# A Strassen-like trunk kernel on one core: one raw tile more, one low less, and more sums done by accumulating transfers

## The chip, the core and the metric

The kernel runs on one core of a Trainium2 chip. The core has five engines with an instruction stream each: TensorE (PE, with its weight loads shown apart as PEld), VectorE (DVE), ScalarE (ACT), GpSimd (POOL) and SyncE (SP). They work from on-chip memory of 128 partitions; sixteen DMA engines move data between it and HBM, and also from one place of it to another. Transfers are issued on queues of SyncE, ScalarE and GpSimd; only those of GpSimd are used here with an add at the destination. The metric is the device time of one launch in microseconds, lower is better.

## The reference

Only layer 0 runs (`DEPTH = 1`): an RMS norm, a stick-breaking attention branch, the residual add, and the final norm. All in float32, with 256 rows, width 4096 and 32 heads of 128.

```python
xn = rms_norm(x, norm_attn)
q, k, v, g = split(xn @ w_in_attn, 4)        # (256, 4096) @ (4096, 16384)
z = q @ k.T / sqrt(128)                      # per head, strictly causal
a = exp(log_sigmoid(z) + suffix sums of log_sigmoid(-z))
h = x + ((a @ v) * silu(g)) @ w_out_attn     # (256, 4096) @ (4096, 4096)
out = rms_norm(h, final_norm)
```

Nearly all arithmetic is in the two products with the weights. The weights are 256 MB for the first product and 64 MB for the second.

## The kernel before

**Products in three passes.** Float32 numbers are split into a high part in the fast format float32r (`wh`, `sh`, `oh`) and a low part that is the rest (`wl`, `sl`, `ol`). One product (`mm3`, line 909) is three matmuls of 512 columns: high x high, low weight x high, high weight x low. For each weight tile ScalarE casts the high part (`cast`, line 556; in the profile `wh<-raw`) and VectorE subtracts it from the raw tile (`low`, line 571; `wl<-raw,wh`).

**Units, steps and parts.** The output columns are cut into 16 input units of 1024 columns (256 each of q, k, v and gate, so two heads) and 4 output units of 1024. A unit goes over the 4096 inner rows in 8 steps. The first unit of each product is plain; the others treat the four 256-column blocks and the two halves of rows as 2 x 2 block products. A seven-product step (`SEVEN_PARTS`, line 97; steps 1, 3, 4, 6 of an input unit, 1, 3, 6 of an output unit) needs seven products for each of its two pairs of inner rows instead of eight, but some of its weight tiles are sums of raw tiles. A mixed step (0, 2, 5) does that for half of its rows, and the remaining steps are ordinary (`EIGHT_PARTS`). A step of seven parts has 14 products, a mixed one 15, an ordinary one 16. A part is the use of one low tile: two products in a seven-product step, four in an ordinary one. Each unit collects its results in seven PSUM banks; at its end VectorE and ScalarE combine the banks (`combine`, line 805; `qk_sb`, `gv_sb`), and the banks are needed again by the next unit.

**Raw tiles and sums.** `load` (line 427) brings in the four quarter tiles of each step on SyncE's queue, two DMAs of 256 KB per tile, into a ring `raw` of `RAW_BUFS` places. In a seven-product step, `add_block` (line 467) adds a second block onto the tile (1, 0) by an accumulating transfer from HBM on GpSimd's queue; it is called T3. That tile is loaded `EARLY` = 2.5 tiles ahead of its turn. `sums` (line 496) then makes further weights in place on VectorE: `near - far`, the second sum and the third sum (`raw<-raw,raw` in the profile). For steps listed in `FOURTH_IN` and `FOURTH_OUT` the third sum is instead an accumulating transfer from on-chip memory to on-chip memory on GpSimd's queue (`raw<-raw`, T4):

```python
fourth = not mixed and parts[a]["s"] in (FOURTH_IN if parts[a]["u"] < OUT0 else FOURTH_OUT)
...
def moved_third():
    yield nc.until(("lows", b))
    x, y = raw[(q, 0, 1)], raw[(q, *near)]
    yield moved("gpsimd", lambda: nc.gpsimd.dma_start(x, y, accum_op=ALU.add), ...)
    yield nc.until(("T4", q), lead=T3_LEAD)
    nc.tell(("sums", g[0]))
    tile_done(q, 0, 1)
    tile_done(q, *near)
```

A raw tile's place comes free when its last cast, low and sum are done. The sixth and seventh part of a seven-product step (`LATE_FROM`, `LATE_BEHIND`) run behind the second part of the step that follows.

**Rings.** Besides `raw` there are `PAIRS` = 6 places for cast tiles and `LOWS` = 6 for lows; a place is given back when TensorE has finished the part. A raw tile and a low both take 4 KB of each partition. `KEPT` (lines 48, 352 to 358): the last parts of the kernel keep their tiles, and their products are ordered by bank, first banks 4 and 5, then 2, then 3, so that row block 1 is complete before row block 0 and its norm and output can begin (`last_h`, line 1208; `finish`, line 1291). `KEPT` must not exceed the number of lows.

**A written order.** The class `Plan` (line 139) plays the kernel through at build time with a cost for each operation and transfer, and writes down the instructions of each engine in the order in which the played engines take them, by a key (how urgent a piece is) among those that are ready. On the chip each engine executes its list strictly in order, waiting on semaphores. So the constants touched by the change act in two ways: some set how many places or transfers there are, and others (`T3_LEAD`, `TEN_WAIT`, `QK_LEAD`, `SPREAD`) only shift the order of the lists. `T3_LEAD` is the time after an accumulating transfer's landing before what needs it may be listed. `TEN_WAIT` (line 399) is the time between an attention matmul's being ready and its being listed on TensorE; `QK_LEAD` (line 1037) the same for a unit's first attention step. A transfer with an add is booked with 1.78 us per 256 KB, a plain one with 0.83 (line 265).

**Attention.** The two heads of a unit are worked out during the next unit: five groups of small matmuls per head on TensorE (`tr`, `z`, the suffix sums into `z`, the gate's transpose, `o`), with ScalarE and VectorE between them. The result goes to HBM (`spill`), and `blocks_of_heads` (line 1064) fetches it back (`p<-spill`, GpSimd's queue) and splits it into the stationary forms `oh` and `ol` of the second product. `SPREAD` says from which half-step on: form `s` is not begun before half-step `int(SPREAD[0] + SPREAD[1] * s)`, counted from the start of the last input unit, of 16 half-steps in a unit.

Of the kernel before, what the change touches and what calls it, by code (L numbers as in the profile page):

```python
# [42 lines left out]

SEVEN_IN, MIX_IN = (1, 3, 4, 6), (0, 2, 5)
SEVEN_AFTER, MIX_AFTER = (1, 3, 6), (0, 2, 5)
RAW_BUFS = 8
PAIRS, LOWS = 6, 6
KEPT = 6
LAST_STEPS = (2, 6, 5, 1, 0, 3, 7, 4)
LATE_FROM, LATE_BEHIND = 4, 1  # L50

SPREAD = (8, 1.1)
HEADS_AHEAD = 3
HEADS_LATER = 12
AHEAD, SUMS_AHEAD = 1.0, 3.0
PIPE = 1
T3_LEAD = 1500
FOURTH_IN, FOURTH_OUT = (1, 3), ()
FOURTH_AHEAD = 6.0
RAW_LEAD = 0  # L60
EARLY = 2.5
TEN_WAIT = 1200
QK_LEAD = 2000
CAST_AHEAD = 3.0
BLOCKS_LATER = 2
OUT_ACT = (1, 4, 7)
# [68 lines left out]
def tensor_ns(n):  # L135
    return 0.4167 * n + 13.4 if n > 128 else 109.0
# [137 lines left out]
def kernel(  # L274
# [76 lines left out]
    n_parts = len(parts)  # L351
    kept = range(n_parts - KEPT, n_parts)
    begun = len(PLAIN_PARTS) * NS
    order = [(n, k) for n in range(begun) for k in range(len(parts[n]["prods"]))]
    order.sort(key=lambda e: (parts[e[0]]["s"], parts[e[0]]["prods"][e[1]][2]))
    order += [(n, k) for n in range(begun, n_parts - KEPT) for k in range(len(parts[n]["prods"]))]
    for banks in ((4, 5), (2,), (3,)):
# [41 lines left out]
    def ten(emit, *n):  # L399
        return nc.work("tensor", 90 + sum(tensor_ns(m) for m in n), emit, nc.here - 1e4, wait=TEN_WAIT)  # L400

# [10 lines left out]
    for name, places in (  # L412
        ("raw", RAW_BUFS), ("w", PAIRS), ("low", LOWS), ("gh", 3), ("one", 1), ("two", 1),
        ("qkh", 1), ("qkl", 1), ("f", 1), ("att", 1), ("heads", 1),
# [12 lines left out]
    def load():  # L427
# [8 lines left out]
        for _, q, t, k in sorted(tiles):  # L436
            if 1 < q < NS:
                yield nc.until(("used", 0, max(HALF * q - LOAD_AHEAD, 0)))
            yield nc.take("raw")
            raw[q, t, k] = wp.tile([P, HG, HALF, CW], F32, tag="raw", name=f"raw{q}_{t}{k}", bufs=RAW_BUFS)  # L440
            if seven[q] and (t, k) == (1, 0):
# [54 lines left out]
    def sums(q):  # L496
# [16 lines left out]

        yield nc.until(("T3", q), lead=T3_LEAD)
        yield nc.until(("lows", a))
# [9 lines left out]
        def moved_third():  # L525
# [5 lines left out]
            )  # L531
            yield nc.until(("T4", q), lead=T3_LEAD)
            nc.tell(("sums", g[0]))
# [358 lines left out]
    def gate(u):  # L892
        yield nc.until(("gv", u))
        g = st["gv", u][:, :, CW:W]
        n = NT * CW
        yield nc.take("qkl")
        l = ap.tile([P, NT, CW], F32, tag="qkl", name=f"gl{u}")
        yield act(lambda: nc.scalar.activation(l, g, AF.Abs), n)
        yield act(lambda: nc.scalar.activation(l, l, AF.Exp, scale=-1.0), n)
        yield act(lambda: nc.scalar.activation(l, l, AF.Ln, bias=1.0), n)  # L900
        yield dve(
            lambda: nc.vector.scalar_tensor_tensor(out=l, in0=g, scalar=0.0, in1=l, op0=ALU.min, op1=ALU.subtract), n
        )
        yield act(lambda: nc.scalar.activation(l, l, AF.Exp), n)
        yield dve(lambda: nc.vector.tensor_tensor(out=g, in0=g, in1=l, op=ALU.mult), n)
        nc.give("qkl")
        nc.tell(("gate", u))
# [127 lines left out]
    def heads(u):  # L1035
        nc.start(gate(u))
        yield nc.until(("qk", u), lead=QK_LEAD)
        for i in range(HG):
# [21 lines left out]
    def later_than(u, s):  # L1060
        s = int(SPREAD[0] + SPREAD[1] * s)
        return "used", u + s // FINE, s % FINE
# [56 lines left out]
    def fetch():  # L1119

        yield nc.until("loaded", ("h", NJ - 3, 1))
        for c in AWAY:
            yield nc.take("raw")
            both = wp.tile([P, HG, HALF, CW], F32, tag="raw", name=f"back{c}", bufs=RAW_BUFS)
            for t in range(NT):
# [318 lines left out]
```

## Time and profile before

| | us |
|---|---|
| three timed runs | 1742.09, 1746.84, 1747.45 |
| their median | 1746.84 |
| the profiled execution | 1742.72 |
| its span, first to last instruction | 1741.0 |

The profile shows one execution. It gives, for each engine, busy time and instructions; for windows of time, each engine's busy time with the number of instructions, then the granted TensorE clock as a share of full speed, the share of the sixteen DMA engines' time that was busy (it can come out a little over 1), and the rate in GB/s; for each group of instructions, which engine waited for what (in all, how often, longest); for DMA issues, their size and the median time from issue to landing; and the chain of work that ended last. Matmuls are pipelined, so one that lasts 0.39 us can be followed by the next after less. A wait in square brackets behind a timeline row is the idle time of that engine before the instruction, with what ended it. Since nearly every instruction is issued through one helper, all have line 158; rows are told apart by their tiles, written as out<-in.

### The profile page before, as it was taken

How to read it: one execution, taken by the hardware profiler on the slowest of the kernel's cores; microseconds unless marked ns; L12 is line 12 of the kernel's file. 1: busy time of each engine (PE TensorE's matmuls, PEld its weight loads, DVE VectorE, ACT ScalarE, POOL GpSimd, SP SyncE). 2: the span in 40 equal slices, each digit the busy share in tenths (PEclk: the TensorE clock that was granted, in tenths of full speed). 3: DMA queues.
4: the chain of work that ended last, by engine and by line, in shares of the span. 5: the costliest groups of instructions: out<-in, count | busy, mean ns of one | idle time of the engine just before them, and what ended most of it. 6: DMA issues, size and time to landing. Idle time of an engine off the chain costs nothing.

```text
span 1741.0 us, 23954 instructions
## 1 busy us (share of the span) xinstructions
PE 1713.9 (98%) x7690; PEld 1407.4 (81%) x7690; DVE 1630.2 (94%) x1872; ACT 1227.0 (70%) x1599; POOL 209.1 (12%) x224
## 2 busy tenths in 40 slices
PE   9999999999999999999999999999999999999997
PEld 6888888888888888888787878787888778888885
DVE  7889999999999999999999999999999987899997
ACT  7876777676777676767686767676767665666664
POOL 0010111011101011111111111111111022011100
PEclk9999999999999999999999999999999999999998
DMA  9998989888989898988888988889898778798886
GB/s 302 316 251 242 254 243 241 239 252 254 243 253 248 249 239 254 238 252 236 250 242 246 237 250 232 247 235 260 232 258 236 254 251 241 232 290 243 261 255 230
DMA packets 240543, 434.84 MB, mean 250 GB/s; under 512 B 25472, under 2 KB 45440, under 8 KB 240416
## 3 DMA queue, kind: packets, MB, share of 16 engines
q1 hardware_dynamic: 197616, 354.24, 62.0%
q0 software_dynamic: 41504, 77.22, 24.4%
q10 hardware_dynamic: 1296, 1.85, 0.3%
q8 instruction: 60, 0.98, 0.2%
q14 instruction: 67, 0.55, 0.1%
HBM read 407.52 MB, written 9.96 MB: 240 GB/s over the span
## 4 chain that ended last, share of the span: by engine, by line
PE 65%; DVE 13%; DMA 11%; issue 5%; ACT 4%; SPq 1%; POOL 0%; ACTq 0%; DVEq 0%; POOLq 0%
PE acc L158 62%; DMA raw<-in_w_in_dram 8%; DVE wl L158 8%; ACT wh L158 3%; DVE raw L158 3%; PE z L158 2%; DMA xres<-in_x_dram 1%; PE o L158 1%; SPq L158 1%; DMA p<-spill 1%; PE tr L158 1%; DMA raw<-in_w_out_dram 1%; ACT f L158 0%; DVE qk_sb L158 0%; DVE h L158 0%
## 5 line engine op out<-in xcount | busy, mean ns | idle before, releaser
L158 ACT CAST wh<-raw 128x1024 fp32r<-128x1024 f32 (+1 forms) x959 | 941.9, 1021 | 393.1 <-DMA raw<-in_w_in_dram 201.2
L158 DVE TENSOR_TENSOR wl<-raw,wh 128x1024 fp32r<-128x1024 f32 (+1 forms) x959 | 1100.8, 1184 | 60.3 <-ACT wh L158 57.0
L158 PE MATMUL acc<-wh,sh 128*128 128x512 f32 x1883 | 751.6, 399 | 4.3 <-DVE qk_sb L158 2.5
L158 PE MATMUL acc<-wl,sh 128*128 128x512 f32 x1883 | 735.9, 391 | 6.7 <-DVE wl L158 6.0
L158 PE MATMUL acc<-wh,sl 128*128 128x512 f32 x1883 | 735.6, 391 | 0.0
L158 PEld LDWEIGHTS acc<-wl,sh 128*128 128x128 f32 x1883 | 354.5, 188 | 85.2 <-DVE wl L158 15.7
L158 PEld LDWEIGHTS acc<-wh,sh 128*128 128x128 f32 x1883 | 354.2, 188 | 77.0 <-DVE qk_sb L158 5.8
L158 PEld LDWEIGHTS acc<-wh,sl 128*128 128x128 f32 x1883 | 353.8, 188 | 75.5 <-DVE sl L158 0.2
L158 DVE TENSOR_TENSOR raw<-raw,raw 128x1024 f32<-128x1024 f32 (+1 forms) x339 | 326.2, 964 | 2.0
L158 POOL DMA_DIRECT2D raw<-in_w_in_dram x105 | 127.9, 1218 | 931.6 <-DMA raw<-in_w_in_dram 522.9
L158 PE MATMUL acc<-wl,oh 128*128 128x512 f32 x485 | 189.5, 391 | 2.2 <-DVE wl L158 2.1
L158 PE MATMUL acc<-wh,oh 128*128 128x512 f32 x485 | 189.9, 391 | 0.0
L158 PE MATMUL acc<-wh,ol 128*128 128x512 f32 x485 | 188.8, 389 | 0.0
L158 PEld LDWEIGHTS acc<-wl,oh 128*128 128x128 f32 x485 | 91.1, 188 | 23.2 <-DVE wl L158 4.8
L158 PEld LDWEIGHTS acc<-wh,ol 128*128 128x128 f32 x485 | 91.1, 188 | 18.8
L158 PEld LDWEIGHTS acc<-wh,oh 128*128 128x128 f32 x485 | 91.1, 188 | 18.7
L158 ACT ACTIVATE f<-f 128x384 f32<-128x384 f32 x96 | 50.5, 526 | 3.0
L158 POOL DMA_DIRECT2D raw<-raw x30 | 26.5, 882 | 208.9 <-ACT f L158 86.7
L158 ACT CAST oh<-p 128x512 fp32r<-128x512 f32 (+3 forms) x41 | 19.3, 488 | 32.5 <-DVE p L158 16.6
L158 POOL DMA_DIRECT2D raw<-in_w_out_dram x18 | 21.5, 1192 | 136.2 <-DMA raw<-in_w_out_dram 105.4
L158 DVE SCALAR_TENSOR_TENSOR gv_sb<-acc,rin_v,gv_sb 128x512 f32<-128x512 f32 x45 | 33.5, 745 | 0.7
L158 POOL DMA_DIRECT2D p<-spill x41 | 22.9, 567 | 90.4 <-DVE ol L158 84.7
(88 smaller groups left out, 749.3 us busy)
## 6 DMA issues: line engine op xcount, KB each, us to landing
raw<-in_w_in_dram SPq DMA_DIRECT2D x1016, 256.0 KB, 5.0
raw<-in_w_out_dram SPq DMA_DIRECT2D x256, 256.0 KB, 5.1
raw<-in_w_in_dram POOLq DMA_DIRECT2D x60, 512.0 KB, 8.7
raw<-raw POOLq DMA_DIRECT2D x30, 512.0 KB, 6.8
raw<-in_w_in_dram POOLq DMA_DIRECT2D x45, 256.0 KB, 6.3
p<-spill POOLq DMA_DIRECT2D x41, 128.0 KB, 4.7
raw<-in_w_out_dram POOLq DMA_DIRECT2D x9, 512.0 KB, 8.8
xr<-in_x_dram SPq DMA_DIRECT2D x16, 256.0 KB, 5.5
```

What stands on the lines that cost most here:

```text
L158: return self.tc.keep_in_program_order(getattr(self.engine, name)(*args, **kw))
```

## The change

Only constants differ. There is one more raw tile and one low less; the last five parts are reordered instead of six; the third sum of step 4 of the 15 input units that have seven-product steps, and of step 1 of the three such output units, becomes an accumulating transfer; and four constants of the planner are shifted: forms of heads begin two half-steps later, what follows an accumulating transfer is listed 0.5 us later, attention matmuls are listed 0.2 us earlier after being ready, and a unit's first attention step 0.5 us earlier. The change was described with the words "weights of the first product loaded first" as well; the difference between the two files has no line for it.

```diff
-RAW_BUFS = 8
-PAIRS, LOWS = 6, 6
-KEPT = 6
+RAW_BUFS = 9
+PAIRS, LOWS = 6, 5
+KEPT = 5
...
-SPREAD = (8, 1.1)
+SPREAD = (10, 1.1)
...
-T3_LEAD = 1500
-FOURTH_IN, FOURTH_OUT = (1, 3), ()
+T3_LEAD = 2000
+FOURTH_IN, FOURTH_OUT = (1, 3, 4), (1,)
...
-TEN_WAIT = 1200
-QK_LEAD = 2000
+TEN_WAIT = 1000
+QK_LEAD = 1500
```

## The prediction

> **What bounds the kernel now.** I read the busy shares first, then the windows of 100 us, then the waits of the weight loads, the chain, and the timeline where the chain leaves TensorE.
>
> ```profile
> span 1741.0 us, 23954 instructions
> ...
> PE 1713.9 (98%) x7690; PEld 1407.4 (81%) x7690; DVE 1630.2 (94%) x1872; ACT 1227.0 (70%) x1599; POOL 209.1 (12%) x224
> ```
> ```profile
> 0.00:100.00 100.00, 96.05 (x405) 76.35 (x406) 80.04 (x148) 82.66 (x155) 4.83 (x11) 0.98 0.92 304
> 500.00:600.00 100.00, 100.00 (x455) 82.84 (x454) 97.17 (x102) 73.38 (x91) 11.85 (x11) 1.00 0.88 246
> 1100.00:1200.00 100.00, 98.84 (x444) 80.49 (x443) 94.53 (x101) 72.42 (x90) 11.85 (x11) 1.00 0.86 242
> 1300.00:1400.00 100.00, 98.10 (x446) 80.37 (x444) 95.79 (x115) 73.96 (x98) 13.59 (x19) 1.00 0.83 243
> ```
>
> Three resources are nearly full at once: TensorE at 98 to 100 in 100 us, VectorE at 95 to 97, the DMA engines at 0.83 to 0.92 (second last column). From 500 to 600 us TensorE has no hole and VectorE is at its fullest. Where TensorE has holes, VectorE is a little emptier: it is late there because it was held up before. So TensorE sets the end, and what can be won is its holes.
>
> How much is that? A hole shows best in the weight load that ends it (waits of the whole run; then of the window from 97 to 1300 us; then the timeline at one hole):
>
> ```profile
> PEld acc L158 <- DVE wl L158: 20.5, 30, 1.1
> PEld acc L158 <- DVE qk_sb L158: 5.8, 9, 1.1
> ```
> ```profile
> PEld acc L158 <- DVE wl L158: 10.5, 17, 1.1
> ```
> ```profile
> 1111.14 0.39 PE L158 MATMUL acc<-wh,sh 128*128 128x512 f32 x1
> 1111.66 1.22 DVE L158 TENSOR_TENSOR raw<-raw,raw 128x1024 f32<-128x1024 f32 x1
> 1111.80 0.19 PEld L158 LDWEIGHTS acc<-wl,sh 128*128 128x128 f32 x1 [0.69 <-DVE wl L158]
> ```
> ```profile
> 1095.21 5.31 DMA raw<-in_w_in_dram
> ...
> 1115.85 15.82 PE acc L158 x68
> ...
> 1443.06 51.72 PE acc L158 x228
> ```
>
> The last chain line gives the undisturbed pace: 51.72/228 = 0.227 us for a 512-column matmul. At 1111 us the next matmul starts 0.66 us after the one before, so 0.43 us is lost where the weight load waited 0.69: a wait costs 0.26 less than it reads. That makes 20.5 - 30 x 0.26 = 12.7 us behind lows (`wl`), of them 10.5 - 17 x 0.26 = 6.1 in the input units up to 1300 us, and 5.8 - 9 x 0.26 = 3.5 us behind evictions (`qk_sb`): **16.2 us** or 0.9% in all. No change of order can win more.
>
> Where are they? The loss at 1111 us lies in step 6 (a seven-product step) of an input unit. The chain has just come out of a DMA load at 1095; the timeline shows how:
>
> ```profile
> 1099.93 5.37 ACT L158 CAST wh<-raw 128x1024 fp32r<-128x1024 f32 x6 [3.96 <-DMA raw<-in_w_in_dram]
> ...
> 1101.96 5.24 DVE L158 TENSOR_TENSOR wl<-raw,wh 128x1024 fp32r<-128x1024 f32 x5 [1.26 <-ACT wh L158]
> ```
>
> ```profile
> L158 ACT CAST wh<-raw 128x1024 fp32r<-128x1024 f32 (+1 forms) x959 | 941.9, 1021 | 393.1 <-DMA raw<-in_w_in_dram 201.2
> ```
>
> That is no single case: loads hold the casts up for 201 us of the run. ScalarE stands 3.96 us for a raw tile, VectorE then 1.26 us for the cast, and ten microseconds later TensorE has its hole. VectorE cannot make good what it lost, because a seven-product step asks too much of it:
>
> ```profile
> 1339.98 4.63 DVE L158 TENSOR_TENSOR wl<-raw,wh 128x1024 fp32r<-128x1024 f32 x4
> ```
>
> Four in 4.63 us with the last taking 1.22 is one per 1.14 us. A step with four sums on VectorE needs 7 lows and 4 sums, 11 x 1.14 = 12.5 us, against 14 products x 3 x 0.227 = 9.5 us on TensorE. Steps 3, 4 and 6 run it down; steps 7, 0 and 2 refill it.
>
> **The change part by part.**
>
> *Third sums by transfer* (step 4 of 15 input units, step 1 of 3 output units). Removed: 18 VectorE sums of 1.14 us, 20.5 us of VectorE, of which 1.14 per input unit falls just ahead of the losing step 6. The same sum in steps 1 and 3 already goes that way, 30 times. Added are 18 GpSimd issues and their transfers:
>
> ```profile
> raw<-raw POOLq DMA_DIRECT2D x30, 512.0 KB, 6.8
> ```
> ```profile
> q0 software_dynamic: 41504, 77.22, 24.4%
> ```
> ```profile
> 1073.50:1081.60 8.10, 8.10 (x39) 6.75 (x38) 6.67 (x8) 5.02 (x8) 1.19 (x1) 1.00 1.06 269
> 1081.60:1092.10 10.50, 10.50 (x50) 8.69 (x49) 10.21 (x11) 8.74 (x12) 1.21 (x2) 1.00 0.73 207
> 1092.10:1104.30 12.20, 12.20 (x55) 10.13 (x54) 10.72 (x12) 7.81 (x10) 0.59 (x1) 1.00 0.91 266
> 1104.30:1117.00 12.70, 11.68 (x49) 8.72 (x49) 12.15 (x13) 8.61 (x11) 1.16 (x1) 1.00 0.76 214
> ```
>
> The landing takes 6.8 us; the seventh part that needs it runs behind the next step's second part, so six parts lie between, at least 8 us. GpSimd is 12% busy, so the issue is free; behind it on its queue stands the transfer that adds for the next step, which has its own lead of 2.5 tiles. The queue's rate is 0.244 x 1741/77.22 = 5.5 us of all sixteen engines per MB, so a half MB costs 2.9 us of DMA. The windows are steps 3 to 6 of the unit around 1100 us. Step 4 has the room: 0.73 x 10.5 = 7.7 us becomes 10.6, a full share of 1.0. That is the doubt here: loads for steps 5 and 6 fly then, and by how much they land later lies between 0 (they use gaps) and 2.9 us each. I take 1 us, near the low end, since step 5 at 0.91 and step 6 at 0.76 leave room to catch up. For one such transfer alone the Trainium skill (DMA: Bandwidth & Descriptors, Anatomy of one DMA, SWDGE path) gives 2.0 us and the bytes over 436 GB/s, an estimate of 3.2 us; the 6.8 us of the trace is twice that, so by the page it is mostly queueing, and a sum by the page's figure would leave the loads untouched.
>
> *Nine raw tiles.* The loads wait for places, not for orders:
>
> ```profile
> SPq L158 <- DVE wl L158: 703.9, 387, 7.1
> SPq L158 <- DVE raw L158: 182.0, 85, 5.8
> SPq L158 <- DMA raw<-raw: 42.2, 22, 3.9
> ```
>
> SyncE stands some 930 us for a tile to come free. With a ninth each load is issued one release earlier; four tiles per step of 9.5 us make that 2.4 us. It lands that much earlier where the DMA has room, not at all where its share is 1.0. So the 1.26 us of VectorE at 1102 shrinks by between 0 and 1.26; I take half.
>
> *Five lows, kept 5.* The memory stays the same (4 KB per partition each way). A low only needs the sixth place when a sixth cast is already ahead:
>
> ```profile
> ACT wh L158 <- PE acc L158: 110.0, 132, 3.7
> ```
>
> At most 132 times of 959 are the six cast places full, so a low waits at most that often, always while TensorE has five parts (6.8 us or more) ready. What is queued behind it on VectorE, sums and attention, waits with it. Bounds: 0, and the 110 us of that row if every one of these waits came through to TensorE; I take 0.3, near nothing, since five ready parts must first run out. At the end, one part less is reordered: bank 3 keeps 6 products instead of 8 behind row block 1, so its output has 2 x 0.68 = 1.4 us less cover.
>
> ```profile
> 1729.25 0.42 DVE L158 TENSOR_TENSOR h<-acc,h 128x256 f32<-128x256 f32 x1 [1.58 <-PE acc L158]
> 1729.59 0.87 DVE L158 TENSOR_SCALAR h<-h,factor 128x512 f32<-128x512 f32 x2
> 1730.38 0.42 DVE L158 TENSOR_TENSOR h<-acc,h 128x256 f32<-128x256 f32 x1
> ```
>
> Already two scalings of row block 1 stand between the halves of block 0. VectorE had 1.58 us idle before that, so between 0 and 1.4 us come through; I take 0.4.
>
> *Attention earlier* (`TEN_WAIT` 0.2 us less, `QK_LEAD` 0.5 less). TensorE meets these matmuls sooner; the vector and scalar steps before them may not be done.
>
> ```profile
> PEld z L158 <- DVE fl L158: 0.8, 1, 0.8
> PEld o L158 <- ACT gated L158: 0.7, 1, 0.7
> ```
>
> Only a few of 160 groups (32 heads, five each) wait today, so most have margin. Bounds: 0, and 160 x 0.2 = 32 us if none had; I take 1.
>
> *Spread 10.* The output forms of heads start two half-steps later. In the last input unit this takes work away ahead of a loss:
>
> ```profile
> 1373.51 1.28 DVE L158 TENSOR_TENSOR ol<-p,oh 128x512 fp32r<-128x512 f32 x2
> 1374.71 3.49 DVE L158 TENSOR_TENSOR wl<-raw,wh 128x1024 fp32r<-128x1024 f32 x3
> ```
>
> 1.2 us of VectorE leaves step 6 there; it moves to the plain output unit, where VectorE has room. `T3_LEAD` only shifts sums behind their transfers by 0.5 us: nothing, or at worst what one sum costs, 1.1 us.
>
> *Weights first.* No line of the difference touches the loads' keys. The 3.95 us that TensorE misses in the first 100 us stay.
>
> **The sum.** Lows: a relief of 1.14 + 0.63 us stands against holes of at most 1.1 - 0.26 = 0.84 us each, a few in a row: 5 of the 6.1 us up to 1300 go, and 3 of the 6.6 outside it, where the start and the output steps without a new transfer keep theirs: -8. Evictions at unit borders: VectorE comes to them earlier, half of 3.5: -1.7. Given back: loads behind the new transfer 1, lows 0.3, tail 0.4, attention 1. Net -9.7 + 2.7 = **-7.0**. The profiled execution took 1742.72 us (span 1741.0 and 1.7 around it), so 1735.7 on its own base. The four executions known are 1742.1, 1742.7, 1746.8 and 1747.5, mean 1744.8; the median shown, 1746.84, is 4 us above the profiled one. I forecast 1744.8 - 7.0, rounded to **1738**.
>
> **The rivals.**
>
> *All holes go.* The ninth tile and the saved sums add up, nothing is given back: -14 from 1744.8, 1729 to 1732. For it: the window from 500 to 600 has the same work and no hole. Against: the start and the border evictions.
>
> *The DMA takes back what VectorE gives.* Loads behind the transfer land 1 to 2 us later, ScalarE waits longer in step 5, and step 6 loses as today: 1742 to 1749. For it: 3.96 us of ScalarE wait already there. The Trainium skill (Trainium Kernel Development and Optimization, Key Constraints) says that transfers of all queues share the same sixteen engines; the share of 1.06 in step 3, which has its transfer today, agrees.
>
> *Slower: the transfer starves step 5.* It decides from the point where the share of steps 4 and 5 stays at 1.0, so that the whole 2.9 us reaches loads that are cast the moment they land. VectorE gives 1.14 and the ninth tile nothing: 2.9 - 1.1 = 1.8 us late in each of 15 units, +27, less some 5 won in the output units and at the borders: 1744.8 + 22 = 1767. Against: step 4's share of 0.73.
>
> *Slower: the written order.* The planner books 3.6 us of transfer for such a sum (1.78 per 256 KB) where the rate above gives 2.9. Its loads seem later than they are, so attention is put too early among the products; if TensorE waits the 0.2 us at half of the 160 groups, +16 against -8 (the sum without its 1 for attention) makes 1753.
>
> *The words are not in the code.* "Loaded first" is not; it costs nothing either way.
>
> **How the numbers follow.** Forecast (1733 to 1741) 0.47; all holes go 0.20; DMA takes it back 0.18; starving 0.10; order 0.05. Within 0.3% of 1746.84, 5.2 us, is about what a measurement can tell from no change. Faster: 0.47 + 0.20 and a little of the third, 0.69. Same: 0.18. Slower: 0.13. The range must take in all holes gone and the third rival, and leaves out most of the last two: 1726 to 1752.
>
> **What would show it.** Right: waits of weight loads on `wl` fall from 30 to about 12, step 6 of the input units has no hole, ScalarE's 201 us of waits for input loads shrink by a third, `raw<-raw` issues are 48, VectorE's busy time falls by 20 us. Wrong: the loads' landing takes over 1 us longer, with more ScalarE wait in step 5; new weight-load waits on `qkT`, `fl`, `a` or `gated`; VectorE waiting for `acc` before `wl`, which today's list does not have.

## The result and the profile after

| | before | after |
|---|---|---|
| timed runs, us | 1742.09 to 1750.38 (4) | 1724.37 to 1726.44 (4) |
| median, us | 1747.14 | 1724.87 |
| profiled execution, us | 1742.72 | 1724.37 |
| its span, us | 1741.0 | 1722.7 |

The ratio is 0.9879, 95% interval 0.9852 to 0.9905: 1.2% faster. The forecast was 1738 with a range of 1726 to 1752; the direction was right and the gain was about three times the 7 us forecast. The runs also lie closer together, within 2 us where before spread over 8.

The page of the kernel after: span, busy time of each engine, and the chain that ended last.

```profile
span 1722.7 us, 24825 instructions
...
PE 1704.0 (99%) x7690; PEld 1410.6 (82%) x7690; DVE 1615.0 (94%) x1854; ACT 1244.2 (72%) x1599; POOL 225.6 (13%) x242
...
PE 97%; DVE 1%; DMA 1%; SPq 0%; issue 0%; ACT 0%; ACTq 0%; DVEq 0%
```

The chain hardly leaves TensorE any more. VectorE is as full as it was, and works 15 us less in all. The windows of 100 us answer to the three shown of before:

```profile
500.00:600.00 100.00, 100.00 (x455) 83.06 (x454) 95.64 (x100) 73.99 (x89) 13.94 (x13) 1.00 0.91 248
...
1100.00:1200.00 100.00, 100.00 (x455) 83.07 (x454) 96.82 (x104) 74.15 (x91) 13.92 (x13) 1.00 0.91 258
...
1300.00:1400.00 100.00, 100.00 (x457) 83.08 (x457) 97.55 (x133) 75.29 (x100) 16.73 (x26) 1.00 0.85 261
```

TensorE is at 100.00 also where it had holes, and the DMA share rose to 0.91. What the weight loads still wait for (all of the run), after:

```profile
PEld acc L158 <- DVE wl L158: 3.1, 3, 1.5
PEld acc L158 <- ACT wh L158: 2.8, 1, 2.8
```

Three waits on lows instead of 30, and none on evictions. A piece of 42 matmuls recurs once in each unit, and its starts tell the units' length; first of before, then of after (the chain):

```profile
191.02 9.54 PE acc L158 x42
...
363.20 9.54 PE acc L158 x42
...
448.15 9.54 PE acc L158 x42
...
1048.58 9.54 PE acc L158 x42
...
1135.53 9.54 PE acc L158 x42
...
1307.79 9.54 PE acc L158 x42
```
```profile
356.98 9.56 PE acc L158 x42
...
1121.44 9.56 PE acc L158 x42
...
1206.38 9.56 PE acc L158 x42
...
1291.32 9.56 PE acc L158 x42
```

Before, the units differ: one without holes took 84.95 us (from 363.20), one of the worst 86.95 (from 1048.58), and the thirteen between 191.02 and 1307.79 took 85.91 on average, so about 1 us a unit was lost. After, each of the eleven between 356.98 and 1291.32 took 84.94. That is the pace of the matmuls, since TensorE has no hole there.

Why VectorE is no longer late shows in what ScalarE waits for before a cast; after:

```profile
ACT wh L158 <- PE acc L158: 222.6, 349, 3.2
ACT wh L158 <- DMA raw<-in_w_in_dram: 82.1, 58, 2.8
```

Before it was the other way round, 110 us for TensorE to give back a place and 201 us for loads. For the most part the supply now runs full: the casts wait for TensorE. The loads did not become quicker (DMA issues of after, median time to landing last):

```profile
raw<-in_w_in_dram SPq DMA_DIRECT2D x1016, 256.0 KB, 5.5
...
raw<-raw POOLq DMA_DIRECT2D x48, 512.0 KB, 6.0
```

They take longer to land than the 5.0 us that this row shows for before; they are only issued early enough.

One thing became worse. TensorE's last piece of the chain, before and after:

```profile
1703.15 26.07 PE acc L158 x113
```
```profile
1684.41 24.60 PE acc L158 x107
```

TensorE is done at 1729.2 and at 1709.0 us, 20.2 us earlier, but the span is only 18.3 us shorter: the end grew from 11.8 to 13.7 us. VectorE after the last matmuls:

```profile
1709.04 0.42 DVE L158 TENSOR_TENSOR h<-acc,h 128x256 f32<-128x256 f32 x1 [1.42 <-PE acc L158]
1709.38 0.87 DVE L158 TENSOR_SCALAR back<-back,factor 128x512 f32<-128x512 f32 x2
1710.17 0.42 DVE L158 TENSOR_TENSOR h<-acc,h 128x256 f32<-128x256 f32 x1
1710.51 1.27 DVE L158 TENSOR_SCALAR h<-h,factor 128x512 f32<-128x512 f32 x3
```

It stood 1.42 us for bank 3 while five scalings were listed behind that add; the run tail_lead, below, moves the add.

### The profile page after: what moved, and what is told of

Its sections match the earlier page's. It is cut to its first block, busy times and chain, and to the rows that moved or that the text cites. A ratio compares the mean times of both kernels' runs of the same rounds, so it can differ in the third digit from the quotient of the medians.

```text
span 1722.7 us, 24825 instructions
## 1 busy us (share of the span) xinstructions
PE 1704.0 (99%) x7690; PEld 1410.6 (82%) x7690; DVE 1615.0 (94%) x1854; ACT 1244.2 (72%) x1599; POOL 225.6 (13%) x242
## 4 chain that ended last, share of the span: by engine, by line
PE 97%; DVE 1%; DMA 1%; SPq 0%; issue 0%; ACT 0%; ACTq 0%; DVEq 0%
PE acc L158 93%; PE z L158 2%; PE o L158 2%; PE tr L158 1%; DMA raw<-in_w_in_dram 1%; SPq L158 0%; DVE wl L158 0%; DVE h L158 0%; DVE raw L158 0%; ACT h L158 0%; ACT wh L158 0%; DVE xs L158 0%; DVE back L158 0%; DVE sl L158 0%; DVE rout_e L158 0%
## 5 line engine op out<-in xcount | busy, mean ns | idle before, releaser
L158 ACT CAST wh<-raw 128x1024 fp32r<-128x1024 f32 (+1 forms) x959 | 959.3, 1023 | 378.7 <-PE acc L158 222.6
L158 DVE TENSOR_TENSOR raw<-raw,raw 128x512 f32<-128x512 f32 (+1 forms) x321 | 303.6, 952 | 3.5
L158 PEld LDWEIGHTS acc<-wl,oh 128*128 128x128 f32 x485 | 91.1, 188 | 20.2 <-DVE wl L158 1.5
L158 POOL DMA_DIRECT2D raw<-raw x48 | 42.5, 885 | 357.3 <-DVE wl L158 204.6
```

Source lines behind the costliest of these rows:

```text
L158: return self.tc.keep_in_program_order(getattr(self.engine, name)(*args, **kw))
```

## The experiments

Three theories: **A**, supply: the ninth raw tile keeps casts and lows ahead. **B**, relief: the sums taken from VectorE do it. **C**, the four constants of the written order do it. Each run was timed in one group with the kernel before, on the same chip, so across groups the ratios tell more than the medians. The table gathers the medians, and TensorE's busy time from 200 to 1300 us, which lies wholly in the input units (a hole-free window has 1100.00).

| run | raw / cast / low places | sums by transfer, input and output | order | median us | ratio (95%) | PE busy, 200 to 1300 |
|---|---|---|---|---|---|---|
| before | 8 / 6 / 6 | 1,3 and none | old | 1745.5 to 1749.4 by group | 1 | 1094.18 |
| order_only | 8 / 6 / 6 | 1,3 and none | new | 1745.2 | 0.999 (0.997 to 1.001) | 1096.70 |
| sums_only | 8 / 6 / 6 | 1,3,4 and 1 | old | 1728.9 | 0.991 (0.988 to 0.995) | 1099.61 |
| sums_and_order | 8 / 6 / 6 | 1,3,4 and 1 | new | 1739.4 | 0.996 (0.994 to 0.998) | 1096.21 |
| five_lows | 8 / 6 / 5 | 1,3 and none | old | 1735.7 | 0.993 (0.991 to 0.995) | 1098.84 |
| raw8_lows5 | 8 / 6 / 5 | 1,3,4 and 1 | new | 1746.8 | 1.001 (0.999 to 1.002) | 1094.61 |
| ring_only | 9 / 6 / 5 | 1,3 and none | old | 1732.0 | 0.992 (0.989 to 0.995) | 1100.00 |
| nine_pairs5 | 9 / 5 / 6 | 1,3 and none | old | 1730.3 | 0.992 (0.989 to 0.995) | 1100.00 |
| ring_and_order | 9 / 6 / 5 | 1,3 and none | new | 1732.2 | 0.993 (0.990 to 0.995) | 1100.00 |
| out_sums | 9 / 6 / 5 | 1,3 and 1 | new | 1725.1 | 0.987 (0.984 to 0.989) | 1100.00 |
| ring_and_sums | 9 / 6 / 5 | 1,3,4 and 1 | old | 1727.2 | 0.990 (0.987 to 0.992) | 1100.00 |
| after | 9 / 6 / 5 | 1,3,4 and 1 | new | 1724.9 | 0.988 (0.985 to 0.991) | 1100.00 |

**The ring alone.**

```diff
-RAW_BUFS = 8
-PAIRS, LOWS = 6, 6
-KEPT = 6
+RAW_BUFS = 9
+PAIRS, LOWS = 6, 5
+KEPT = 5
```

> The kernel before with nine raw tiles, five lows and five kept parts, nothing else changed. Theory A (supply: the casts wait for loads, and the ninth tile gives VectorE back its lead): most of the gain is here, 1726 to 1733 us, ScalarE's waits for loads fall from 201 us to under 100, VectorE's busy time stays. Theory B (VectorE relief: the 18 sums taken away decide): 1740 to 1747, waits of weight loads on lows stay near 30. Theory C (the written order decides): 1740 to 1750. On the end: if five kept parts are what lengthens the stretch from the last matmul to the end (11.8 us before, 13.9 after), it is about 13.9 here.

As theory A had it: 1732 us. The window of ring_only with TensorE first, and ScalarE's waits:

```profile
200.00:1300.00 1100.00, 1100.00 (x5013) 913.46 (x5012) 1069.17 (x1141) 811.84 (x998) 139.01 (x130) 1.00 0.89 248
```
```profile
ACT wh L158 <- DMA raw<-in_w_in_dram: 49.9, 41, 2.7
```

Every hole of the input units is gone with VectorE as busy as ever (1069 of 1100 us), and the waits for loads fell from 201 to 50 us. Its end was not longer (11.8 us, where the kernel after has 13.7 and not the 13.9 of the expectation), so five kept parts do not lengthen it. But the output product, from its first matmul to TensorE's end, got longer: 345.1 us against 341.0 before and 336.8 after.

**The sums alone, the order alone, both.**

```diff
-FOURTH_IN, FOURTH_OUT = (1, 3), ()
+FOURTH_IN, FOURTH_OUT = (1, 3, 4), (1,)
```

> The kernel before with the third sums of step 4 (input) and step 1 (output) by transfer, eight raw tiles, six lows. Theory B: 1728 to 1735, waits of weight loads on lows fall from 30 to under 12. Theory A: 1738 to 1746, because loads still come late, and the added 47 us of transfers make ScalarE's waits for loads grow over 201 us. The rival of the prediction that the transfer starves step 5: 1750 to 1767.

> The kernel before with SPREAD, T3_LEAD, TEN_WAIT and QK_LEAD of the kernel after. Theories A and B: 1740 to 1747, no difference; the hole of the last input unit near 1372 us shrinks by about 1 us. Theory C: under 1735.

```diff
-SPREAD = (8, 1.1)
-T3_LEAD = 1500
-TEN_WAIT = 1200
-QK_LEAD = 2000
+SPREAD = (10, 1.1)
+T3_LEAD = 2000
+TEN_WAIT = 1000
+QK_LEAD = 1500
```

> The kernel after with eight raw tiles, six lows and six kept parts again. Theory A: 1736 to 1744. Theory B: 1724 to 1730, nearly all of the gain without the ninth tile; and since six parts are kept, the end is 11.8 us long, which could make it faster than the kernel after.

Theory B holds by itself too: with eight tiles the sums alone gave 1728.9, and the input units were full but for 0.39 us of the window. The starving rival did not come; ScalarE's waits for loads fell, where A expected them to grow. The order alone did nothing that can be told from no change, so C falls as a cause by itself. But order and sums together gave 1739.4, ten more than the sums alone: with eight tiles one cannot add up effects. The same waits in sums_only, then in sums_and_order:

```profile
ACT wh L158 <- DMA raw<-in_w_in_dram: 134.4, 97, 5.6
```
```profile
ACT wh L158 <- DMA raw<-in_w_in_dram: 210.3, 138, 5.9
```

A different list lets the loads come late again, and the gain goes with them.

**Ring with sums, ring with order, and the kernel after without its ninth tile.**

> Nine raw tiles, five lows, five kept parts and the sums by transfer, the four constants of the order as before. If the order constants do nothing by themselves (order_only 1745 against 1748): 1724 to 1727, like the kernel after. If they cost what sums_and_order lost against sums_only (10 us in the profiles) and the ninth tile does not cover it: 1715 to 1720. If they are needed beside the ring: 1727 to 1735.

> The kernel after with the third sums as before (steps 1 and 3, none in the output units). Theory A: input units at 84.95 us each, as in ring_only; the output units keep holes, since VectorE is not relieved there: 1729 to 1735. If the order constants cost time by themselves: over 1737.

```diff
-RAW_BUFS = 9
+RAW_BUFS = 8
```

> The kernel after with eight raw tiles, still five lows: the ninth tile alone is taken away. If five lows cost nothing: like sums_and_order, 1735 to 1745. If the sixth low place matters when VectorE is behind: 1745 to 1755, with VectorE waiting for TensorE before lows.

ring_and_sums lies near the kernel after (1727.2 against 1724.9, profiled 1724.70 against 1724.37, and the intervals of the ratios overlap): the order constants are not shown to be needed beside the ring. ring_and_order is what A expected. And raw8_lows5, the whole change but for one tile, is no faster than before:

```profile
200.00:1300.00 1100.00, 1094.61 (x4957) 901.25 (x4956) 1037.77 (x1110) 786.39 (x980) 147.13 (x140) 1.00 0.92 252
```
```profile
ACT wh L158 <- DMA raw<-in_w_in_dram: 184.6, 105, 5.8
```

VectorE works 19 us less in this window than before (1056.67 there), and TensorE still has its holes: in this list, relief without supply is worth nothing.

**Where the sums earn their part.** Step 4's transfer back on VectorE, the output units' kept:

```diff
-FOURTH_IN, FOURTH_OUT = (1, 3, 4), (1,)
+FOURTH_IN, FOURTH_OUT = (1, 3), (1,)
```

> The kernel after with the third sum of step 4 of the input units back on VectorE; only step 1 of the output units is by transfer. ring_only had all input units at 84.96 us and holes in the output units (82.6 to 82.9 each against 80.92). If the ninth tile alone fills the input units and the sums earn their part only in the output units: 1723 to 1727, as the kernel after. If step 4's transfer is needed as well: 1728 to 1733, as ring_and_order.

The same as the kernel after. Two chain lines of ring_and_order, then of out_sums, at the end of the input units and at TensorE's end:

```profile
1292.35 9.56 PE acc L158 x42
...
1691.03 25.96 PE acc L158 x113
```
```profile
1292.45 9.56 PE acc L158 x42
...
1686.08 24.55 PE acc L158 x107
```

At 1292 us they are level; TensorE ends at 1717.0 and at 1710.6. So three transfers in the output units are worth 6.4 us beside nine tiles, and the fifteen in the input units nothing that the medians can tell (1725.1 without them, 1724.9 with them). Part of the 6.4 only repairs: the output product takes 343.7 us in ring_and_order, 337.3 in out_sums and 341.0 in the kernel before, so nine tiles by themselves made it longer. Why they do was not found.

**The ninth tile or the fifth low?**

```diff
-PAIRS, LOWS = 6, 6
-KEPT = 6
+PAIRS, LOWS = 6, 5
+KEPT = 5
```

> The kernel before with five lows and five kept parts and nothing else. The prediction took 0.3 us for the missing place. raw8_lows5 lost 7 us against sums_and_order, which has six: if the place costs that by itself, 1750 to 1757 here, with VectorE waiting for TensorE before lows. If it costs only together with the other edits: 1745 to 1749.

A miss for both expectations: a place less, and 14 us faster by the medians. Waits for loads stayed long (174 us), holes stayed (20 waits on lows, 12.6 us). Paying for the ninth tile with a cast place instead:

```diff
-RAW_BUFS = 8
-PAIRS, LOWS = 6, 6
-KEPT = 6
+RAW_BUFS = 9
+PAIRS, LOWS = 5, 6
+KEPT = 5
```

> The kernel before with nine raw tiles paid for with a place for cast tiles instead of a low (five cast places, six lows, five kept parts). If the ninth tile is what ring_only won with: input units at 85.0 us each, 1728 to 1736. If ring_only won with its five lows (five_lows alone gave 1736): like before, 1742 to 1750, and holes in the input units stay.

```profile
200.00:1300.00 1100.00, 1100.00 (x5014) 913.91 (x5013) 1071.58 (x1141) 820.88 (x999) 139.12 (x130) 1.00 0.89 248
```

The input units are full with six lows as well, so it is the ninth tile that fills them. With `PAIRS, LOWS = 5, 5` and a tenth:

> The kernel after with a tenth raw tile, paid for with the sixth place for cast tiles. If the supply is already enough with nine (input units stand at 84.94 us, the pace of the matmuls): 1723 to 1728. If five cast places are too few, with ScalarE's lead cut: 1730 to 1745, and waits of ScalarE for TensorE over 300 us.

1729.8 us (0.989, 0.987 to 0.992): the window is full as with nine, so more supply is worth nothing there. The 5 us against the kernel after lie elsewhere: the output product begins 3.4 us later and takes 341.0 us instead of 336.8, and the end is 1.9 us shorter. Whether the tenth tile or the lost cast place costs them was not separated.

**Too many transfers.**

```diff
-FOURTH_IN, FOURTH_OUT = (1, 3, 4), (1,)
+FOURTH_IN, FOURTH_OUT = (1, 3, 4, 6), (1, 3)
```

> The kernel after with the third sums of all four seven-product steps of the input units and of steps 1 and 3 of the output units by transfer: 18 further transfers, 52 us more of DMA time by the rate of the prediction (2.9 each). The prediction's rival: once the DMA engines stay full, loads come late and TensorE stands: 1735 to 1760, ScalarE's waits for loads over 150 us. If the ninth tile covers this too: 1723 to 1727.

1767.4 us, 1.011 (1.008 to 1.014), slower than before and outside both ranges of the expectation. The waits of SyncE before a load and of the weight loads:

```profile
SPq L158 <- DMA raw<-raw: 111.6, 61, 6.5
```
```profile
PEld acc L158 <- DVE wl L158: 22.0, 22, 1.3
PEld acc L158 <- ACT wh L158: 20.7, 17, 4.9
```

The starving rival has the same size, 1767, by chance, since its price is paid in another place than it named: ScalarE's waits for loads stay at 85 us. The raw places are held until the transfers land, 112 us of SyncE's time against 16 in the kernel after, and TensorE waits for casts themselves, up to 4.9 us. The transfers hardly land later (median 6.4 us of 66, against 6.0 of 48 in the kernel after), which speaks for their place in the written order; it was not tried by itself.

**Freeing places without a tile.** In the kernel before, and in raw8_lows5:

```diff
-EARLY = 2.5
+EARLY = 1.0
```

> The kernel before with EARLY 1.0 instead of 2.5: the tile that receives the accumulating transfer of a seven-product step is loaded 1.5 tiles later, so it holds its place for less time and the other tiles share more of the eight. Supply theory: loads of the other tiles are issued some 2 to 4 us earlier, fewer waits of ScalarE for loads (201 us to under 150), 1730 to 1740 without a ninth tile. If that transfer then lands too late: over 1750, ScalarE waiting for it instead. If only the order of the lists matters: anywhere from 1729 to 1748, with unchanged waits for loads.

> raw8_lows5 (the kernel after with eight raw tiles, 1747 us) with EARLY 1.0. Supply theory: clearly under 1747, 1730 to 1740. If the five lows are what costs there: no change, 1742 to 1750.

1769.3 us (1.013, 1.009 to 1.017) and 1805.9 us (1.035, 1.028 to 1.041), both slower, against what the supply theory said; the first is in the range of its second alternative, a transfer that comes too late. Waits of SyncE in early_one:

```profile
SPq L158 <- DMA raw<-in_w_in_dram: 97.5, 108, 3.9
SPq L158 <- DMA raw<-raw: 84.4, 26, 7.2
```

Places are now held by transfers that have not landed (34 and 42 us before). It seems that the tile that receives the adding transfer needs its lead; the two runs speak neither for nor against the supply of the other tiles.

**The end.** In the kernel after, and, in the run called candidate, together with `FOURTH_IN, FOURTH_OUT = (1, 3), (1, 3)`:

```diff
-                yield nc.until(("full", u, 3))
+                yield nc.until(("full", u, 3), lead=1500)
```

> The kernel after, with the add of the last bank listed 1.5 us later at the end, so that the scalings of row block 1 stand ahead of it on VectorE. In the kernel after VectorE stood 1.42 us for that bank while five scalings waited behind it. If that is what made the end 13.9 us instead of 11.8: 1722 to 1724. If the end is set by the output transfers: no change, 1724 to 1726.

> The kernel after with the third sums of steps 1 and 3 by transfer in the output units and of steps 1 and 3 alone in the input units (12 transfers fewer than after), and the end as in tail_lead. One hole of 1.2 us is left in the last output unit of after, near 1683 us; if it closes and the end stays at 12.5 us: 1721 to 1724. If the ends differ by chance only: 1724 to 1727.

tail_lead: 1724.18 us (1723.35 to 1724.82), 0.988 (0.986 to 0.991), 0.7 us under the kernel after and not told apart from it, since the two were not timed side by side. In its profile the end is 12.3 us instead of 13.7, but TensorE ends 1.8 us later. candidate: 1729.4 us, outside both its ranges; it differs from out_sums by this edit and three further output transfers, and its output product takes 341.3 us against 337.3. No version was shown to beat the kernel after.

## Why the prediction was wrong

- *TensorE sets the end, and its holes are what can be won.* Right: the chain is 97% TensorE, and the input units stand at the matmuls' own pace.
- *The size of the holes, 16.2 us.* Too small. The step took 0.26 off each wait and overlooked that TensorE starts slowly again. Before, at the hole that the prediction used:

```profile
1111.80 0.50 PE L158 MATMUL acc<-wl,sh 128*128 128x512 f32 x1 [0.27 <-DVE wl L158]
1112.13 0.39 PE L158 MATMUL acc<-wh,sl 128*128 128x512 f32 x1
```

  The next matmul follows after 0.33 us instead of 0.227, so each hole costs 0.10 more: 39 of them, 3.9 us, and 20.1 in all. TensorE's end came 20.2 us earlier. That the two agree so well is in part luck: the kernel after keeps three such waits, worth 2.6 us by the same working, so about as much was won outside this list. "No change of order can win more" was thus false by the size of one term.
- *The ninth tile: 0 to 1.26 us of relief, half taken.* This is the step that failed most, and with it the term -8 for lows. The tile was counted as one release, once. The runs show it as what fills the input units: all nine runs with nine or ten tiles and at most 18 further transfers, the kernel after among them, stand at 1100.00 from 200 to 1300 us, whatever else differs, and no run with eight does. The output product begins at 1388.2 us before, at 1372.2 after and at 1373.6 in ring_only: 15.9 us won ahead of it, 14.6 of them by the ring alone. The prediction took one late load and one earlier release; the lack is there all along. In each 100 us from 200 to 1300 the casts wait 11.7 to 23.0 us for loads before, and 3.4 to 9.0 after, where the casts wait for TensorE instead (349 times in all). How a late load makes a later release late was argued and not followed tile by tile; nor does each such wait make a hole, since the unit from 363.20 us has none.
- *The sums: -8 together with the tile, by 1.14 us of VectorE in each input unit.* Right as a cause (sums_only), but in the kernel after the input units' transfers are worth nothing measurable beside the ninth tile, and the three in the output units 6.4 us. Against before, the output product is 4.3 us shorter; 3 were taken for all holes outside the input window. VectorE's busy time fell by 15 us and not by 20.
- *Evictions: half of 3.5.* All of it went.
- *Given back: 1 for loads, 0.3 for lows, 1 for attention, 0.4 for the end.* The loads do land later (5.5 us for 5.0), hidden by the lead. No attention matmul waits in the list of after. Of the signs of being wrong that the prediction named, one came, VectorE waiting for TensorE before a low (after):

```profile
DVE wl L158 <- PE acc L158: 16.0, 19, 2.3
```

  It cost nothing in the input units, where TensorE has no hole. The end cost 1.9, above the bound of 1.4: ring_only shows that it isn't the fifth kept part, and tail_lead, with an end of 12.3, speaks for where the scalings are listed.
- *The rival "all holes go"* (1729 to 1732, chance 0.20) is what happened, 4 to 7 us lower than priced, because of the restarts and because 14 of 16.2 was still a part. *Starving* and *the written order* did not come; six_sums shows that more transfers would have been too many. The Trainium skill (Trainium Kernel Development and Optimization, Key Constraints) has all queues share sixteen engines. No run here shows that by itself: the loads' median landing is 5.3 us in sums_only against 5.0 before, but also 5.3 in ring_only, which has no transfer more.
- *Weights first:* TensorE has 96.00 us of the first 100, as before.
- The base: the four executions averaged 1744.8, the later median is 1747.1. With holes the time depends on when loads land; without them it hardly does. That is argued from the spread, 8 us and 2, and was not tried by itself.

Open: why five_lows and sums_only gain 14 and 19 us by the medians with eight tiles, and the order takes 10 of that away again. All eight-tile runs with `EARLY` 2.5, the kernel before among them, lie between 1729 and 1749; which property of a list decides was not found.

## What to carry to other kernels

Where an engine that sets the end has small holes that come from far up (a load, a cast, a subtraction), price a further buffer by what the whole ring lacks over a period, not by the one release that it moves: once the supply runs full, the holes go together, and several cures that each work alone do not add up. Before adding relief, see which wait turns round, from "for loads" to "for the last engine". And with an order written ahead, time a constant in the version in which it is to stay.

## What the runs showed of the hardware

- TensorE after a hole: 0.33 us to the next matmul instead of 0.227, in a stretch whose granted clock is 1.00.
- Adding transfers within on-chip memory landed in 6.0 us (median of 48) where there were 30 that took 6.8, although the DMA share rose from 0.86 to 0.91 in the window from 1100 to 1200 us. That the further transfers are why is not shown: ring_only, with the 30 alone and nine tiles, has 5.8 us, and sums_only, with 48 and eight tiles, 6.6.
